# A hybrid encoder's delta rule: one tile per chunk for the loaded keys and the turned b and k

## Chip, cores, metric

One NeuronCore of a Trainium2 chip runs the whole program. The metric is the device time of one execution in microseconds; the table below gives the median of three runs.

## What is computed

The reference is an encoder of two layers over 1,024 tokens with 16 learned meta tokens in front (L = 1040), width 1,024. Each layer has one combined input projection, a latent attention over 4 heads (group A), a delta-rule recurrence over 8 heads of width 64 in both directions (group B), an output projection, a layer norm, and a mixture of 32 experts with a second layer norm. The part that matters here is the recurrence of group B, run once forward and once backward per layer:

```python
def step(S, inp):
    r_t, w_t, k_t, v_t, kk_t, b_t = inp
    sa = jnp.einsum('bhvk,bhk->bhv', S, kk_t)
    S = S * w_t[:, :, None, :] - sa[..., None] * b_t[:, :, None, :] + v_t[..., None] * k_t[:, :, None, :]
    return S, jnp.einsum('bhvk,bhk->bhv', S, r_t)
```

## The kernel before

The program runs layer by layer: input projection, attention, delta rule together with the output projection, router, experts. Everything is float32; products that need full precision are made of three matmuls on rounded halves (`mm3`, L200).

**The delta rule** (`rwkv`, L1449) works in chunks of 64 positions. The padded sequence has 17 chunks, and 4 pairs of heads lie on the two halves of the 128 partitions. A step of the recurrence is one chunk in one direction. `steps` (L1715) takes the directions in turn: forward chunk 0, backward chunk 16, forward chunk 1, and so on, 34 steps in the first layer and 33 in the second. Two neighbouring steps, one of each direction, are a **job** (L1717), 17 jobs per layer. The jobs' products don't depend on the recurrence; they have four stages:

- `grams` (L1479) loads T (keys kk and r, decayed) and BK (b and k) of both chunks from DRAM on SP's DMA queue (L1493, L1495, L1498), and makes the products of BK and T on TensorE (L1509), two PSUM tiles "e" for each chunk. VectorE masks one half of each product back into the other half of T (L1514); ScalarE copies the other half into AA (L1515). GpSimd masks the part AR of AA (L1521). ScalarE scales BK (L1524), TensorE turns it (L1528), and ScalarE copies the result into BT (L1529).
- `blocks` (L1532) inverts the diagonal 16x16 blocks of A on VectorE, mostly for two jobs at a time.
- `levels` (L1563) joins the blocks to the whole inverse Y (L1578 to L1602).
- `chain` (L1619) is the recurrence itself, step after step: T times the ring tile (L1640, and L1647 for the output), Y times that (L1658), copies into the ring (L1659, L1660), BT times the ring for the next state (L1664), the state into the next ring (L1667), and AR times the ring into the output (L1671), which L1674 or L1676 adds up in `yt`. `new_ring` (L1607) loads a ring tile's values four steps ahead.

**Buffers.** T lives in pools rwt0 and rwt1, AA and BT in rws0 and rws1, each with two buffers; jobs 0, 1, 4, 5, ... use the first pair of pools, jobs 2, 3, 6, 7, ... the second. So job j+4 takes the T, AA and BT tiles of job j, and the first instruction that writes into such a tile waits for the last readers of the tile of before: for T these are L1640 and L1647 of job j, for BT L1664, for AA L1671 and `levels`. One T tile holds both chunks of a job (128 x 2 x 4 x 2 x 128 float32, 8 KB per partition). BK has two buffers in a pool of its own. The "e" tiles have two buffers in PSUM, and the output projection that runs beside the delta rule (`attended`, L951, matmuls at L201 to L203, results taken at L969 and L992) uses the same two.

**Order.** The loop of L1742 issues, for each j, the chain of job j, the levels of job j+1, the grams of job j+3, the blocks, and one or two portions of the output projection. That order gives priorities; a planner in the compiler, with its own model of every instruction's time, then fixes each engine's order (L1772). It lets a later stage's instruction go ahead where it takes the earlier ones to be not ready. On the chip each engine and each DMA queue works through its fixed order, so an instruction that waits holds up what stands behind it on its engine. The experts' stage has an order written by hand (L1404) and is not touched.

Of the kernel before, what the change touches and what calls it, by code (L numbers as in the profile page):

```python
# [11 lines left out]
F32 = mybir.dt.float32  # L12
# [3 lines left out]
AF = mybir.ActivationFunctionType  # L16
OP = mybir.AluOpType
# [1431 lines left out]
def rwkv(tc, li, last, K, P, pc, kr_d, bk_d, bon_d, g_dram, vt_d, yT, mhalf, kept, side, ready):  # L1449

    nc = tc.nc
    V = nc.vector
# [9 lines left out]
    HALF = (lo, hi)  # L1462

    def bank():
        return pp.tile([128, 512], F32, name="m")
# [13 lines left out]
    def grams(runs, sv):  # L1479


        U = 4 * sum(n for _, _, n in runs)

        T = sv[0].tile([128, U, 2, 128], F32, name="T")
        BK = kb.tile([128, U, 2, 64], F32, name="BK")

        at, u0 = [], 0
        for d, c0, n in runs:
            us = slice(u0, u0 + 4 * n)
            at += [(d, c0 + u // 4, u % 4) for u in range(4 * n)]  # L1490
            u0 += 4 * n
            for o, h in enumerate(HALF):
                nc.sync.dma_start(T[h, us, o], kr_d[d, h, c0:c0 + n].rearrange("p c i x -> p (c i) x"))  # L1493
            cs = bk_d[d, :, c0:c0 + n].rearrange("p c i (a t) -> p (c i) a t", a=2)
            nc.sync.dma_start(BK[lo, us], cs[lo])  # L1495
            for a in range(2):

                nc.sync.dma_start(BK[hi, us, 1 - a], cs[hi, :, a])  # L1498
        AA = sv[1].tile([128, U, 128], F32, name="AA")
        A, AR = AA[:, :, :64], AA[:, :, 64:]  # L1500
        BT = sv[1].tile([128, U, 2, 64], F32, name="BT")


        for q0 in range(0, U, 4):
            q = slice(q0, q0 + 4)
            ps = [pe.tile([128, 4, 128], F32, name="e") for _ in HALF]
            for u in range(4):
                for o, h in enumerate(HALF):
                    nc.tensor.matmul(ps[o][:, u], BK[h, q0 + u].rearrange("p a t -> p (a t)"), T[h, q0 + u, o],  # L1509
                                     start=True, stop=True)  # L1510
            mask = K(f"mask{at[q0][0]}")
            for o in range(2):
                a, b = HALF[o], HALF[1 - o]
                V.tensor_tensor(T[b, q, o], ps[o][b], mask[b, None, :].to_broadcast([64, 4, 128]), op=OP.mult)  # L1514
                nc.scalar.activation(AA[a, q], ps[o][a], AF.Copy)  # L1515
        u0 = 0
        for d, c0, n in runs:
            us = slice(u0, u0 + 4 * n)
            u0 += 4 * n
            m = K("rev") if d else K("mask0")[:, 64:]  # L1520
            nc.gpsimd.tensor_tensor(AR[:, us], AR[:, us], m[:, None, :].to_broadcast([128, 4 * n, 64]), op=OP.mult)  # L1521

        for u in range(U):
            nc.scalar.activation(BK[:, u], BK[:, u], AF.Copy, scale=pc[:, at[u][0], at[u][2], at[u][1]:at[u][1] + 1])  # L1524
        for q0 in range(0, U, 4):
            ps = bank().rearrange("p (a b) -> p a b", a=4)
            for u in range(4):
                nc.tensor.transpose(ps[:, u], BK[:, q0 + u].rearrange("p a t -> p (a t)"), ident)  # L1528
            nc.scalar.activation(BT[:, q0:q0 + 4].rearrange("p u o x -> p u (o x)"), ps, AF.Copy)  # L1529
        return T, A, AR, BT, {x: u for u, x in enumerate(at)}  # L1530

    def blocks(As, E):  # L1532
# [74 lines left out]
    def new_ring(d, c):  # L1607

        rings[d, c] = ring = ch.tile([128, 4, 2, 64], F32, name="ring", bufs=AHEAD + 2)
        for o in range(2):  # L1610
            nc.sync.dma_start(ring[HALF[1 - o], :, o],
                              vt_d[64 * c:64 * c + 64].rearrange("p (i o x) -> p i o x", i=4, o=2)[:, :, o])
        if c == orders[d][0]:
            for o in range(2):
                nc.gpsimd.memset(ring[HALF[o], :, o], 0.0)
# [1 line left out]
    shared = {}  # L1617

    def chain(job, s, Y):  # L1619
        T, _, AR, BT, units = s  # L1620
        for d, c in job:
            ring = rings.pop((d, c))
            x = steps.index((d, c))
            if x + AHEAD < len(steps):
                new_ring(*steps[x + AHEAD])
            more = c != orders[d][-1]
            want = not (last and c == 0)
            pos = orders[d].index(c)

            def un(i):  # L1630
                return units[d, c, i]


            if x % 2 == 0:
                shared["tu"] = pq.tile([128, 2, 4, 64], F32, name="tu")
                shared["st"] = pq.tile([128, 2, 4, 64], F32, name="st")
            tu, ps = shared["tu"][:, x % 2], shared["st"][:, x % 2]
            for i in range(4):
                for o in range(2):
                    nc.tensor.matmul(tu[HALF[o], i], T[:, un(i), o, 0:64], ring[:, i, o], start=True, stop=True)  # L1640
            t0 = ch.tile([128, 4, 64], F32, name="t0", bufs=2)
            nc.scalar.activation(t0, tu, AF.Copy)
            if want:
                py = pq.tile([128, 4, 64], F32, name="y", bufs=2)
                for i in range(4):
                    for o in range(2):
                        nc.tensor.matmul(py[HALF[o], i], T[:, un(i), o, 64:], ring[:, i, o], start=i == 0, stop=False,  # L1647
                                         skip_group_check=True)
            if more:
                nring = rings[d, orders[d][pos + 1]]  # L1650
                sp = ch.tile([128, 4, 64], F32, name="sp", bufs=2)
                for o in range(2):
                    a = HALF[o]
                    nc.gpsimd.tensor_tensor(sp[a], ring[a, :, o], pc[a, d, :, c:c + 1].to_broadcast([64, 4, 64]),  # L1654
                                            op=OP.mult)
            for i in range(4):
                for o in range(2):
                    nc.tensor.matmul(tu[HALF[o], i], Y[HALF[o], un(i)], t0[HALF[o], i], start=True, stop=True)  # L1658
            nc.scalar.activation(ring[lo, :, 0], tu[lo], AF.Copy, scale=-1.0)  # L1659
            nc.scalar.activation(ring[hi, :, 1], tu[hi], AF.Copy, scale=-1.0)  # L1660
            if more:
                for i in range(4):
                    for o in range(2):
                        nc.tensor.matmul(ps[HALF[o], i], BT[:, un(i), o], ring[:, i, o], start=True, stop=True)  # L1664
                for o in range(2):
                    a = HALF[o]
                    V.tensor_tensor(nring[a, :, o], ps[a], sp[a], op=OP.add)  # L1667
            if want:
                for i in range(4):
                    for o in range(2):  # L1670
                        nc.tensor.matmul(py[HALF[o], i], AR[HALF[o], un(i)], ring[HALF[o], i, o], start=False,  # L1671
                                         stop=True, skip_group_check=True)
                if c in touched:
                    V.tensor_tensor(yt[:, c], yt[:, c], py, op=OP.add)  # L1674
                else:
                    nc.scalar.activation(yt[:, c], py, AF.Copy)  # L1676
                touched[c] = touched.get(c, 0) + 1
                tile_ = [0] if c == 0 else [(c - 1) // 2 * 2 + 1, (c - 1) // 2 * 2 + 2]
                if all(touched.get(x, 0) == 2 for x in tile_):
                    ends.append(tile_)  # L1680
# [39 lines left out]
    def stage(k, j):  # L1720
        if j < len(jobs):
            job = jobs[j]
            if k == 0:
                cs = [sorted(c for d, c in job if d == e) for e in range(2)]
                gs[j] = grams([(d, c[0], len(c)) for d, c in enumerate(cs) if c], svs[j % 4 // 2])
            elif k == 1:
                js = [0] if j == 0 else [x for x in (j, j + 1) if j % 2 and x < len(jobs)]
                if js:
                    Ys.update(zip(js, blocks([gs[x][1] for x in js], V if j == 0 else nc.gpsimd)))
            elif k == 2:  # L1730
                levels(gs[j][1], Ys[j])
            else:
                chain(job, gs.pop(j), Ys.pop(j))
# [42 lines left out]
```

## Time and profile before

| | |
|---|---|
| median of 3 runs | 3237.86 us (3231.32 to 3243.92) |
| the profiled execution | 3243.99 us, span 3242.1 us |
| TensorE matmul busy | 2737.0 us, 84% of the span |
| VectorE busy | 2174.9 us, 67% |
| ScalarE busy | 1658.0 us, 51% |
| GpSimd busy | 1040.8 us, 32% |
| mean granted TensorE clock | 0.881 of full speed |

The profile is of one execution. PE is TensorE's matmul, PEld its weight loads, DVE VectorE, ACT ScalarE, POOL GpSimd, SPq the DMA queue of SyncE. A busy TensorE is not one at its peak, since the matmuls' ends are modelled. Times within the trace are microseconds from the span's start; the first layer's delta rule runs from about 631 to 1122, the second's from about 2240 to 2722. A name in brackets behind a row, as [1.18 <-DMA T<-kr_d], is the engine's idle time just before it and what ended it.

### The profile page before, as it was taken

What the parts mean: (1) busy time and instruction counts of PE and PEld (TensorE: products, weight loads), DVE (VectorE), ACT (ScalarE), POOL (GpSimd) and SP (SyncE); (2) the same over time, 40 slices, a digit from 0 to 9 for tenths busy, and PEclk for the clock granted to TensorE, in tenths of its full rate; (3) what the DMA queues carried; (4) which work ended last, traced back from release to release, by engine and by line L of the source; (5) the groups of instructions that cost most, each with busy time, mean ns of one, the idle gap of its engine ahead of it and who ended that gap; (6) DMA issues with size and microseconds to landing.
All of it is one profiled execution on the core that took longest, in us unless ns stands there. A gap on an engine that the chain in (4) does not pass through costs nothing. (4 is left out here: it accounts for less than half of the span.)

```text
span 3242.1 us, 57910 instructions
## 1 busy us (share of the span) xinstructions
PE 2737.0 (84%) x22160; PEld 2231.9 (69%) x22160; DVE 2174.9 (67%) x4257; ACT 1658.0 (51%) x3604; POOL 1040.8 (32%) x1049
## 2 busy tenths in 40 slices
PE   5989899979998978888498997999699889788882
PEld 4878687768776765666388876888587767566551
DVE  7667554566677668888656747445666666787885
ACT  5334454544445447777433435445344434577772
POOL 3656211143336411111245632112433544111111
PEclk9999899968978979999799988988787879799996
DMA  5345610233323449999724565102432325688875
GB/s 175 103 144 174 200 35 21 66 108 105 91 78 96 144 176 327 323 318 314 252 70 136 161 205 182 40 14 75 130 101 67 95 81 185 235 310 313 309 278 223
DMA packets 342732, 523.76 MB, mean 162 GB/s; under 512 B 110733, under 2 KB 263309, under 8 KB 315809
## 3 DMA queue, kind: packets, MB, share of 16 engines
q1 hardware_dynamic: 234832, 399.11, 38.2%
q10 hardware_dynamic: 93280, 87.04, 7.9%
q0 software_dynamic: 14336, 33.84, 2.9%
q8 instruction: 176, 2.88, 0.4%
q14 instruction: 108, 0.88, 0.1%
HBM read 406.57 MB, written 129.84 MB: 165 GB/s over the span
## 5 line engine op out<-in xcount | busy, mean ns | idle before, releaser
L1221 DVE TENSOR_TENSOR w_lo<-raw,w_hi 128x512 fp32r<-128x512 f32 x768 | 472.8, 684 | 9.3 <-ACT w_hi L1217 9.1
L1217 ACT ACTIVATE w_hi<-raw 128x512 fp32r<-128x512 f32 x768 | 412.1, 620 | 0.0
L201 PE MATMUL pj<-hT_hi,w_hi 128*128 128x352 f32 (+1 forms) x912 | 303.3, 333 | 3.7 <-ACT k L437 2.7
L202 PE MATMUL pj<-hT_lo,w_hi 128*128 128x352 f32 (+1 forms) x912 | 301.4, 331 | 2.8 <-DVE hT_lo L212 2.8
L203 PE MATMUL pj<-hT_hi,w_lo 128*128 128x352 f32 (+1 forms) x912 | 299.7, 329 | 0.0
L1273 POOL DMA_INDIRECT y_rows<-y,VS x64 | 64.5, 1007 | 617.6 <-ACT y L1272 595.7
L201 PE MATMUL ph<-w_hi,xT_hi 128*96 128x512 f32 x512 | 226.9, 443 | 3.4 <-ACT w_hi L1217 3.4
L202 PE MATMUL ph<-w_lo,xT_hi 128*96 128x512 f32 x512 | 222.7, 435 | 1.3 <-DVE w_lo L1221 1.3
L203 PE MATMUL ph<-w_hi,xT_lo 128*96 128x512 f32 x512 | 221.4, 432 | 0.0
L1509 PE MATMUL e<-T,BK 64*128 64x128 f32 x1072 | 171.8, 340 | 38.3 <-DMA T<-kr_d 21.0
L212 DVE TENSOR_TENSOR pT_lo<-tr,pT_hi 128x512 fp32r<-128x512 f32 (+2 forms) x176 | 101.4, 592 | 127.5 <-ACT pT_hi L209 127.0
L201 PEld LDWEIGHTS pj<-hT_hi,w_hi 128*128 128x128 f32 x912 | 176.6, 194 | 14.6 <-issue 6.9
L202 PEld LDWEIGHTS pj<-hT_lo,w_hi 128*128 128x128 f32 x912 | 176.6, 194 | 9.3 <-issue 4.9
L1509 PEld LDWEIGHTS e<-T,BK 64*128 64x128 f32 x1072 | 145.0, 234 | 54.1 <-ACT AA L1515 19.8
L203 PEld LDWEIGHTS pj<-hT_hi,w_lo 128*128 128x128 f32 x912 | 176.1, 193 | 5.0 <-issue 4.3
L1514 DVE TENSOR_TENSOR T<-e,cc 64x512 f32<-64x512 f32 x134 | 92.2, 688 | 89.3 <-PE e L1509 86.9
L1654 POOL TENSOR_TENSOR sp<-ring,pc 64x256 f32<-64x256 f32 x126 | 85.2, 676 | 165.9 <-DVE ring L1667 145.1
L209 ACT ACTIVATE pT_hi<-tr 128x512 fp32r<-128x512 f32 (+2 forms) x176 | 86.7, 517 | 94.3 <-PE tr L873 92.9
L1551 DVE TENSOR_TENSOR sb<-sb,dg 128x16 f32<-128x16 f32 (+8 forms) x270 | 107.1, 397 | 40.5 <-POOL dg L1543 33.4
L203 PEld LDWEIGHTS ph<-w_hi,xT_lo 128*96 128x96 f32 x512 | 93.1, 182 | 43.1 <-issue 3.2
L201 PEld LDWEIGHTS ph<-w_hi,xT_hi 128*96 128x96 f32 x512 | 93.4, 182 | 42.5 <-ACT w_hi L1217 4.1
L202 PEld LDWEIGHTS ph<-w_lo,xT_hi 128*96 128x96 f32 x512 | 93.1, 182 | 40.2 <-DVE w_lo L1221 2.3
(422 smaller groups left out, 7635.3 us busy)
## 6 DMA issues: line engine op xcount, KB each, us to landing
raw<-in_w_moe_dram SPq DMA_DIRECT2D x192, 1024.0 KB
w_raw<-in_w_in_dram SPq DMA_DIRECT2D x38, 512.0 KB
T<-kr_d SPq DMA_DIRECT2D x134, 128.0 KB
ys<-y_rows SPq DMA_DIRECT2D x16, 1024.0 KB
a_d<-ht SPq DMA_DIRECT2D x25, 512.0 KB
h_rows<-h ACTq DMA_DIRECT2D x24, 512.0 KB
kr_d<-KR ACTq DMA_DIRECT2D x16, 576.0 KB
bk_d<-BK ACTq DMA_DIRECT2D x16, 576.0 KB
```

Source lines behind the costliest of these rows:

```text
L201: nc.tensor.matmul(o, a.hi, b.hi, start=start, stop=False)
L202: nc.tensor.matmul(o, a.hi, b.lo, start=False, stop=False)
L203: nc.tensor.matmul(o, a.lo, b.hi, start=False, stop=stop)
L209: hi = nc.scalar.activation(dst.hi, src, AF.Copy)
L212: return hi, e_lo.tensor_tensor(dst.lo, src, dst.hi.bitcast(F32), op=OP.subtract)
L1217: nc.scalar.activation(w.hi[:, cs], raw[:, cs], AF.Copy)
L1221: V.tensor_tensor(w.lo[:, cs], raw[:, cs], w.hi[:, cs].bitcast(F32), op=OP.subtract)
L1273: nc.gpsimd.indirect_dma_start(out=rows, out_offset=bass.IndirectOffsetOnAxis(ap=vs, axis=0), in_=y[:n], in_offset=None, bounds_check=2 * ...
L1509: nc.tensor.matmul(ps[o][:, u], BK[h, q0 + u].rearrange("p a t -> p (a t)"), T[h, q0 + u, o], start=True, stop=True)
L1514: V.tensor_tensor(T[b, q, o], ps[o][b], mask[b, None, :].to_broadcast([64, 4, 128]), op=OP.mult)
L1551: V.tensor_tensor(sb[:, :, cs], sb[:, :, cs], dg[:, :, t_:t_ + 1].to_broadcast([128, n, w]), op=OP.mult)
L1654: nc.gpsimd.tensor_tensor(sp[a], ring[a, :, o], pc[a, d, :, c:c + 1].to_broadcast([64, 4, 64]), op=OP.mult)
```

## The change

T and BT become dictionaries with one tile for each chunk, each of half the size of before, and each of these tiles has four buffers in its pool where there were two. The memory taken is the same. Each chunk's two loads of T go to its own tile. BK, AA and Y stay as they are, one tile for the two chunks of a job. The products, masks, copies and the chain are the same instructions on the new tiles.

```diff
@@ grams
-        T = sv[0].tile([128, U, 2, 128], F32, name="T")
+        T, BT = {}, {}
         BK = kb.tile([128, U, 2, 64], F32, name="BK")
...
-            for o, h in enumerate(HALF):
-                nc.sync.dma_start(T[h, us, o], kr_d[d, h, c0:c0 + n].rearrange("p c i x -> p (c i) x"))
+            for c in range(c0, c0 + n):
+
+                T[d, c] = sv[0].tile([128, 4, 2, 128], F32, name="T", bufs=4)
+                for o, h in enumerate(HALF):
+                    nc.sync.dma_start(T[d, c][h, :, o], kr_d[d, h, c])
...
         AA = sv[1].tile([128, U, 128], F32, name="AA")
         A, AR = AA[:, :, :64], AA[:, :, 64:]
-        BT = sv[1].tile([128, U, 2, 64], F32, name="BT")
...
+            Tq = T[at[q0][:2]]
             for u in range(4):
                 for o, h in enumerate(HALF):
-                    nc.tensor.matmul(ps[o][:, u], BK[h, q0 + u].rearrange("p a t -> p (a t)"), T[h, q0 + u, o],
+                    nc.tensor.matmul(ps[o][:, u], BK[h, q0 + u].rearrange("p a t -> p (a t)"), Tq[h, u, o],
                                      start=True, stop=True)
...
-                V.tensor_tensor(T[b, q, o], ps[o][b], mask[b, None, :].to_broadcast([64, 4, 128]), op=OP.mult)
+                V.tensor_tensor(Tq[b, :, o], ps[o][b], mask[b, None, :].to_broadcast([64, 4, 128]), op=OP.mult)
...
-            nc.scalar.activation(BT[:, q0:q0 + 4].rearrange("p u o x -> p u (o x)"), ps, AF.Copy)
+            bt = BT[at[q0][:2]] = sv[1].tile([128, 4, 2, 64], F32, name="BT", bufs=4)
+            nc.scalar.activation(bt.rearrange("p u o x -> p u (o x)"), ps, AF.Copy)
@@ chain
-        T, _, AR, BT, units = s
+        Ts, _, AR, BTs, units = s
         for d, c in job:
+            T, BT = Ts[d, c], BTs[d, c]
...
-                    nc.tensor.matmul(tu[HALF[o], i], T[:, un(i), o, 0:64], ring[:, i, o], start=True, stop=True)
+                    nc.tensor.matmul(tu[HALF[o], i], T[:, i, o, 0:64], ring[:, i, o], start=True, stop=True)
...
-                        nc.tensor.matmul(ps[HALF[o], i], BT[:, un(i), o], ring[:, i, o], start=True, stop=True)
+                        nc.tensor.matmul(ps[HALF[o], i], BT[:, i, o], ring[:, i, o], start=True, stop=True)
```

## Rows read from the trace of the kernel before

**Rows 1.** Windows of both stages: us; busy (count) of PE, PEld, DVE, ACT, POOL; clock, DMA
```profile
631.40:1122.00 490.60, 434.89 (x6257) 359.76 (x6256) 338.29 (x880) 225.51 (x520) 205.03 (x214) 0.85 0.34 96
2240.00:2722.00 482.00, 421.81 (x5943) 352.85 (x5941) 314.99 (x849) 214.09 (x498) 193.11 (x206) 0.82 0.34 95
```

**Rows 2.** TensorE's waits, first stage then second: us in total, times, longest
```profile
PE tu L1640 <- DMA ring<-vt_d: 10.5, 1, 10.5
PE e L1509 <- DMA T<-kr_d: 10.0, 7, 2.5
PE e L1509 <- ACT AA L1515: 7.8, 8, 2.6
...
PE tu L1640 <- DMA ring<-vt_d: 16.4, 1, 16.4
PE e L1509 <- DMA T<-kr_d: 10.9, 6, 2.4
PE e L1509 <- ACT AA L1515: 9.5, 7, 3.7
```

**Rows 3.** Timeline of TensorE within one job: start, us, instructions of one kind merged
```profile
719.03 1.12 PE L1647 MATMUL y<-ring,T 128*64 128x64 f32 x16
...
738.97 0.56 PE L1647 MATMUL y<-ring,T 128*64 128x64 f32 x10
739.58 0.33 PE L1664 MATMUL st<-ring,BT 128*64 128x64 f32 x2
...
741.34 1.93 PE L1509 MATMUL e<-T,BK 64*128 64x128 f32 x8 [1.18 <-DMA T<-kr_d]
...
743.87 1.11 PE L1664 MATMUL st<-ring,BT 128*64 128x64 f32 x14
744.92 1.11 PE L1671 MATMUL y<-ring,AA 64*64 64x64 f32 x14
...
746.42 1.12 PE L1640 MATMUL tu<-ring,T 128*64 128x64 f32 x16
```

**Rows 4.** Timeline of SP's DMA queue before and in the same job
```profile
703.02 0.47 SPq L1495 DMA_DIRECT2D BK<-bk_d  x1
...
733.24 0.52 SPq L1495 DMA_DIRECT2D BK<-bk_d  x1
...
737.79 3.38 SPq L1493 DMA_DIRECT2D T<-kr_d  x4
```

**Rows 5.** Timeline of ScalarE in the same job
```profile
746.35 0.58 ACT L1515 ACTIVATE AA<-e 64x512 f32<-64x512 f32 x1
...
753.82 0.60 ACT L1529 ACTIVATE BT<-m 128x512 f32<-128x512 f32 x1 [0.26 <-PE m L1528]
...
758.92 0.38 ACT L1660 ACTIVATE ring<-tu 64x256 f32<-64x256 f32 x1
```

**Rows 6.** Windows around three waits for T, columns as in rows 1
```profile
740.20:741.30 1.10, 0.00 (x0) 0.00 (x0) 1.07 (x4) 0.00 (x0) 0.00 (x0) 1.00 0.62 183
...
741.30:762.00 20.70, 20.66 (x189) 17.43 (x190) 14.54 (x37) 9.24 (x22) 5.72 (x6) 0.51 0.28 74
...
888.40:903.00 14.60, 14.58 (x160) 12.69 (x161) 6.46 (x21) 5.54 (x13) 2.13 (x3) 0.50 0.10 26
938.90:950.00 11.10, 11.10 (x140) 9.89 (x140) 6.39 (x17) 4.54 (x11) 2.11 (x3) 0.53 0.18 44
```

**Rows 7.** Timeline of TensorE behind a wait for L1515
```profile
800.67 1.16 PE L1509 MATMUL e<-T,BK 64*128 64x128 f32 x8 [1.39 <-ACT AA L1515]
...
803.36 1.86 PE L1509 MATMUL e<-T,BK 64*128 64x128 f32 x7
```

**Rows 8.** SP's own waits from 700 to 1020: us in total, times, longest
```profile
SPq L1493 <- PE tu L1658: 4.0, 5, 1.3
```

**Rows 9.** Timeline of TensorE, side work ahead of the chain (first of 24, then L1664)
```profile
758.21 0.79 PE L201 MATMUL e<-wo_hi,ya_hi 128*128 128x512 f32 x1
...
765.62 0.69 PE L1664 MATMUL st<-ring,BT 128*64 128x64 f32 x16
```

More of the change, by code (lines that the diff above doesn't have):

```diff
@@ L1646, in chain @@
                     for o in range(2):
-                        nc.tensor.matmul(py[HALF[o], i], T[:, un(i), o, 64:], ring[:, i, o], start=i == 0, stop=False,
+                        nc.tensor.matmul(py[HALF[o], i], T[:, i, o, 64:], ring[:, i, o], start=i == 0, stop=False,
                                          skip_group_check=True)
```

## The prediction

> **What bounds the kernel now.** The chain of waits that ended last only shows the last stage, so I read the delta-rule stages by windows first. There are two, one per layer, 490.6 and 482.0 us long, together 30% of the span; TensorE is busy 89% and 88% of them at a mean granted clock of 0.85 and 0.82 [rows 1]. All else in the program is left as it is. So the change can only win or lose here: TensorE's idle time is 490.6 - 434.9 = 55.7 and 482.0 - 421.8 = 60.2 us, and a clock below 1.
>
> Next the waits of TensorE in these stages [rows 2]. The largest single ones are the first ring loads (10.5 and 16.4 us, once per layer), which no part of the change touches. Then comes what it does touch: the key products of L1509 wait for the load of T, 10.0 us in 7 waits and 10.9 us in 6, together 20.9 us. The same products wait 7.8 and 9.5 us for L1515, which empties their PSUM bank into AA.
>
> Third, one job in order of time. T of job j is last read by L1647 of its second chunk (start 738.97, sixteen matmuls) [rows 3]. The four loads of T for job j+4 start on SP at 737.79 and take 3.38 us, the first of them held up [rows 4]. L1509 starts at 741.34 after 1.18 us of idle TensorE, eight matmuls at 1.93 us; the recurrence's own L1664 of the same step, which had begun at 739.58, goes on only at 743.87, and the next job's L1640 follows at 746.42 [rows 3]. So the load is issued when the old T tile comes free and is used at once: here the buffer, not the transfer's length, sets the time. The other operand is early: BK for these products was loaded from 703.02 on, and 733.24 is already the next job's [rows 4].
>
> **The change, part by part.** *Counts:* 134 loads of T, the products, masks and copies stay; only what they wait for differs. No instruction is added and none is longer, so the direct cost is nil on every queue.
>
> *T.* The first chunk's T is free when L1647 of the first chunk ends, start 719.03 plus 1.12 [rows 3], instead of about 739.5: 19 us earlier. Its two loads can go out on SP in the stretch before the BK loads of 733.24 [rows 4]. L1509 of that chunk then finds T in place, and the 13 waits go: -20.9 us at most [rows 2]. The second chunk's T still comes free at 739.5, but only two loads instead of four are issued then, and its products run behind the first chunk's, at 747 or later in this job, well after they land. I cost that at nothing; the cover is the first chunk's products and, if these have already run, the wait would be back, 1.6 us each (20.9/13).
>
> *What is late next.* L1515 writes AA, still one tile for two chunks with two buffers. It can't start before L1671 of the second chunk, 744.92 plus 1.11, and it does start at 746.35 [rows 3, 5]. So the products' results leave PSUM no earlier, and the second half of the products meets the wait for L1515, whose present mean is 17.3/15 = 1.15 us [rows 2]. I let half of the 13 jobs pay it: 6 x 1.15 = +7. Net -14 us. The ends: -21 (none pays), and 0 (each pays as much as it saved).
> The Trainium skill ("Perfetto Trace Analysis", the section Optimization Strategy) reads a gap that keeps coming back on the engine that should be busy as a sign of too few or too large buffers for the next tile; by that rule alone the smaller T tiles would give back the whole 20.9 us, and the sum would be 7 us lower than mine. The rows show a second tile, AA, with the same users and the same two buffers, which the rule doesn't set against the first; so I keep the +7.
>
> *TensorE's clock.* In the gap of 740.2 to 741.3 the granted clock is 1.00 with nothing running; in the 20.7 us behind it, 0.51, with TensorE busy throughout; 14.6 us at 0.50 and 11.1 at 0.53 follow two other waits of this kind [rows 6]. That is the 1.2 GHz level. At the 2.4 GHz level these three stretches would lose up to half, 10 + 7 + 5 = 22 us, if TensorE's work alone set their length. The ends for the clock are 0 and about -50 us, this sum carried to seven of the 13 waits (22 x 7/3 = 51). But the clock falls behind waits that stay, too: after 1.39 us for L1515 at 800.67, seven products at 803.36 take 1.86 us [rows 7]. I take -10, nearer to nothing because the wait for L1515 is still there.
>
> *SP.* The early load of the first chunk can stand in SP's order ahead of BK, ring and y loads. If L1647 runs late, these wait behind it. SP's waits for T now are 4.0 us in 5 cases [rows 8]; BK is 30 us early and rings are four steps ahead, so nothing of that reaches TensorE. *BT.* Its copy starts at 753.82 [rows 5], behind L1664 of both chunks at 743.87; an earlier release of half of it moves nothing: 0. *First loads of a stage and the last releases:* the first products wait for the attention's end, not for T: 0.
>
> Sum against the profiled execution, 3243.99 us (span 3242.1 and 1.9 around it): -14 - 10 = -24, 3220. The median of the runs is 6.1 us lower, so **3214 us**.
>
> **The rivals.**
> *The wait only moves (no difference).* AA's release at 746 stays the tightest tie, and the order that the planner writes down is fixed for the run: with the wait for T gone, TensorE waits for L1515 in the same gap. For it: L1515 follows L1671 by 1.4 us in this job [rows 3, 5]. Against: in the gap at 740.2, L1664 of the chain stands behind the products, and that goes with T alone. Time: 3238 less 0 to 8, about 3234.
>
> *Early products hold the PSUM banks (slower).* Products of a chunk take both "e" banks, and keep them until L1515, which waits for AA. Today they start about 5 us ahead of AA's release; with T free at 720 they can start up to 20 us ahead. The output projection's side work needs the same two banks; two halves, 24 matmuls, run from 758.21 to 765.62, 3.7 us per half, and there they already stand ahead of the chain's L1664, whose input was ready at 759.3 (758.92 plus 0.38) [rows 5, 9]. If a half that now fills a gap is pushed behind AA's release, it lies on the chain. With one half in every second of 28 jobs that is 14 x 3.7 = +52, less the 24 saved: +28, 3266. It decides from about seven halves on (24/3.7). For it: two banks and three users. Against: the side work of an earlier round is ordered ahead of later products wherever both are ready.
> The Trainium skill ("Trainium Kernel Development and Optimization", Best Practices) warns to mind PSUM pressure, since evacuation is not made faster by what speeds up the matmuls; that is this rival, and no row yet shows the banks as the cause of a late projection.
>
> *The clock comes back in full (much faster).* The gaps go and with them most half-speed stretches: -14 - 36 = -50, 3188. For it: TensorE is busy in the whole of each such stretch. Against: the fall behind a wait that stays [rows 7].
>
> **How the numbers follow.** Forecast 0.42, no difference 0.27, banks held 0.20, full clock 0.11. About 0.5% (16 us) is what a measurement of this kernel can tell from no change. The forecast's own range is 3204 to 3228; a sixth of its chance, 0.07, lies within 0.5%. Faster: 0.35 + 0.11 = 0.46. Same: 0.27 + 0.07 = 0.34. Slower: 0.20. The range begins at the full-clock case, 3187, and ends at 3258, seven tenths of the way from 3238 to the slower case; the rest of that case and a little below 3187 are left out.
>
> **What would show it.** Right: TensorE's waits of L1509 for T fall from 20.9 us to under 4; the two T loads of a job's first chunk are issued apart from the second's, some 15 us earlier; L1664 of a second chunk is no longer cut in two by products; the stages are 470 to 480 us long with a clock of 0.86 or more. Wrong: the waits for L1515 grow from 17.3 to 30 us or more (the wait moved); the side work of L201 to L203 stands later in its job and waits for L1515 (banks held); or the waits for T stay, with the second chunk's products now first behind their load. A changed order far from T, such as longer first ring waits, would make the prediction wrong for a reason that it doesn't hold.

## The result, and the profile after

The changed kernel takes 3213.12 us (median of 6 runs, 3206.73 to 3217.06), the kernel before 3240.89 us (median of 6, 3231.32 to 3253.51). The ratio is 0.9911 with a 95% interval of 0.9888 to 0.9934, so it is faster by 0.9%, by more than the 0.5% that can be told from no change. The profiled execution took 3206.73 us, its span 3205.0 us, at a mean granted clock of 0.897 (before: 3243.99, 3242.1 and 0.881).

The windows of both stages after the change (length; busy time and count of PE, PEld, DVE, ACT, POOL; clock, DMA share, GB/s):

```profile
633.00:1108.00 475.00, 411.44 (x6203) 339.39 (x6202) 331.41 (x863) 220.55 (x515) 200.22 (x212) 0.87 0.34 96
2235.00:2682.00 447.00, 381.87 (x5907) 317.38 (x5907) 309.81 (x844) 208.80 (x486) 192.38 (x204) 0.89 0.36 101
```

Against [rows 1] the windows are 15.6 and 35.0 us shorter and the clock is up from 0.85 and 0.82; they do not hold quite the same work (6203 matmuls against 6257, and 5907 against 5943). But TensorE's idle time, length less PE busy, is 63.6 and 65.1 us where it was 55.7 and 60.2. The change was to remove idle time, and there is more of it; the busy time fell.

To compare kernels I narrow the windows to the recurrence itself, from the first to the last T-times-ring product (L1640 before, L1645 after) of each layer; the first ring load's wait lies ahead of it. First the kernel before:

```profile
669.60:1108.00 438.40, 397.24 (x5932) 328.08 (x5932) 300.95 (x785) 196.69 (x458) 181.71 (x191) 0.85 0.35 99
2284.00:2721.90 437.90, 394.18 (x5736) 328.87 (x5736) 282.60 (x764) 191.00 (x445) 175.90 (x186) 0.83 0.34 98
```

The same windows after:

```profile
673.70:1099.60 425.90, 379.45 (x5932) 312.51 (x5932) 298.24 (x785) 195.37 (x458) 179.72 (x191) 0.87 0.34 98
2271.90:2678.90 407.00, 359.65 (x5734) 298.33 (x5736) 281.08 (x763) 189.64 (x446) 176.12 (x186) 0.90 0.36 103
```

The counts of matmuls agree within two, so it is the same work. Together the two windows fell from 876.3 to 832.9 us (-43.4): PE busy from 791.4 to 739.1 (-52.3), idle from 84.9 to 93.8 (+8.9). The rest of the program was 6.3 us longer in this execution (2372.1 against 2365.8), which makes the span's 37.1. The execution profiled after the change is the fastest of its six, so this is more than the medians' 27.8 us.

TensorE's waits after the change in the two stages, first then second (us in total, times, longest):

```profile
PE e L1512 <- ACT AA L1518: 9.3, 8, 3.8
PE y L1652 <- DVE ring L1672: 7.5, 4, 5.0
PE y L1652 <- DVE yt L1679: 5.8, 4, 3.3
PE y L1652 <- ACT AA L1518: 2.0, 1, 2.0
PE m L1603 <- ACT W L1599: 1.2, 3, 0.5
...
PE y L1652 <- DVE yt L1679: 11.0, 5, 8.0
PE e L1512 <- ACT AA L1518: 8.7, 7, 3.2
PE m L1603 <- ACT W L1599: 7.6, 7, 5.6
PE y L1652 <- ACT AA L1518: 2.8, 3, 1.2
PE y L1652 <- DVE ring L1672: 2.0, 3, 0.9
```

No wait for T is left where there were 20.9 us of them [rows 2]. The key products (L1512 now) wait 18.0 us for L1518, practically the 17.3 of before. What grew are the waits of the output product and the levels, which in the kernel before stood as follows (first stage, then second):

```profile
PE y L1647 <- DVE yt L1674: 5.6, 4, 3.2
PE m L1599 <- ACT W L1595: 0.7, 2, 0.5
...
PE y L1647 <- DVE yt L1674: 6.5, 4, 2.6
PE y L1647 <- DVE ring L1667: 2.7, 1, 2.7
PE m L1599 <- ACT W L1595: 2.3, 3, 1.6
```

The output product waited 5.6 + 6.5 + 2.7 = 14.8 us for VectorE and now waits 7.5 + 5.8 + 11.0 + 2.0 = 26.3; the levels' wait for W went from 3.0 to 8.8. These two groups alone take back 17.3 of the 20.9 us. Another 4.8 us of the output product's waits are put down to L1518, and none were before.

One job of the first layer, at the place of [rows 3], on TensorE after the change (start, length, merged instructions, idle time before):

```profile
739.61 0.56 PE L1652 MATMUL y<-ring,T 128*64 128x64 f32 x10
740.10 1.16 PE L1512 MATMUL e<-T,BK 64*128 64x128 f32 x16
...
741.71 0.68 PE L1669 MATMUL st<-ring,BT 128*64 128x64 f32 x14
...
743.54 0.69 PE L1645 MATMUL tu<-ring,T 128*64 128x64 f32 x16
746.20 1.05 PE L1652 MATMUL y<-ring,T 128*64 128x64 f32 x16 [1.97 <-ACT AA L1518]
747.17 2.38 PE L1512 MATMUL e<-T,BK 64*128 64x128 f32 x16
```

The same place on SP's queue:

```profile
721.99 1.84 SPq L1496 DMA_DIRECT2D T<-kr_d  x2
...
738.45 1.91 SPq L1496 DMA_DIRECT2D T<-kr_d  x2
```

Each chunk has its own pair of loads. Counted from the start of the stage, the products at 740.10 are the eleventh chunk's and use the eleventh pair, 721.99 to 723.83, there 16 us earlier; those at 747.17 are the twelfth chunk's and use the pair that ended at 740.36, 7 us earlier. Before, the four loads ended at 741.17 and the products began at 741.34 [rows 3, 4]. Sixteen records of products (the trace has two for each matmul, so this is one chunk's eight) now take 1.16 us without a gap, where eight records took 1.93 at the lower clock, and the next job's first product starts at 743.54, not 746.42 [rows 3]. Then a wait of another kind comes, 1.97 us at 746.20. It is put down to L1518, though L1652 doesn't read AA; by the same timeline L1672 writes the ring tile that it reads from 745.64 on, 0.87 us in two halves. The clock around it (columns as in the windows above):

```profile
739.50:746.00 6.50, 4.73 (x113) 4.02 (x108) 6.15 (x19) 3.49 (x9) 0.56 (x1) 1.00 0.58 157
746.00:754.80 8.80, 8.53 (x76) 7.30 (x77) 8.24 (x22) 4.95 (x13) 4.76 (x6) 0.62 0.11 32
754.80:760.00 5.20, 5.20 (x37) 3.92 (x35) 3.65 (x7) 1.35 (x3) 0.69 (x2) 0.99 0.21 50
```

Where [rows 6] had 20.7 us at 0.51 there are now 8.8 us at 0.62. The clock still falls behind a wait, but later and for less.

### The profile page after: what moved, and what is told of

Same layout as the page of the kernel before. It is cut to its first block, busy times and chain, and to the rows that moved or that the text cites. A ratio compares the mean times of both kernels' runs of the same rounds, so it can differ in the third digit from the quotient of the medians.

```text
span 3205.0 us, 57957 instructions
## 1 busy us (share of the span) xinstructions
PE 2675.5 (83%) x22160; PEld 2177.7 (68%) x22160; DVE 2172.9 (68%) x4257; ACT 1653.0 (52%) x3604; POOL 1040.0 (32%) x1049
## 5 line engine op out<-in xcount | busy, mean ns | idle before, releaser
L201 PE MATMUL pj<-hT_hi,w_hi 128*128 128x352 f32 (+1 forms) x912 | 303.3, 333 | 3.7 <-ACT k L437 2.7
L201 PE MATMUL ph<-w_hi,xT_hi 128*96 128x512 f32 x512 | 226.1, 442 | 3.4 <-ACT w_hi L1217 3.4
L201 PEld LDWEIGHTS pj<-hT_hi,w_hi 128*128 128x128 f32 x912 | 176.7, 194 | 14.9 <-issue 6.9
L1512 PE MATMUL e<-T,BK 64*128 64x128 f32 x1072 | 150.7, 320 | 19.4 <-ACT AA L1518 18.0
L1512 PEld LDWEIGHTS e<-T,BK 64*128 64x128 f32 x1072 | 125.7, 215 | 33.1 <-ACT AA L1518 20.6
L1517 DVE TENSOR_TENSOR T<-e,cc 64x512 f32<-64x512 f32 x134 | 92.3, 689 | 59.3 <-PE e L1512 56.4
L201 PEld LDWEIGHTS ph<-w_hi,xT_hi 128*96 128x96 f32 x512 | 93.1, 182 | 42.4 <-issue 4.7
```

The lines of the kernel that those rows point to most:

```text
L201: nc.tensor.matmul(o, a.hi, b.hi, start=start, stop=False)
L1517: V.tensor_tensor(Tq[b, :, o], ps[o][b], mask[b, None, :].to_broadcast([64, 4, 128]), op=OP.mult)
```

## The experiments

Three questions: is it T's tie or BT's, or merely another order (the planner writes a new order for every kernel); is AA the next tie; and is it the idle time or the clock that pays. A chip's own median of before ran from 3254.81 to 3262.77 us in these runs, so ratios to before on the same chip are compared. All results in one table. *Recurrence*, *PE busy* and *idle* are sums over the two windows of each profiled execution; *lower level* is worked out as twice the length times (1 - clock), since every record of the granted clock stands at one of two levels, 1.0 or half of it (as the clock is read with two digits, this is good to about 9 us); *T waits* are TensorE's in the whole program.

| run | ratio to before (95%) | recurrence | PE busy | idle | clock | lower level | T waits |
|---|---|---|---|---|---|---|---|
| before | 1 | 876.3 | 791.4 | 84.9 | 0.85, 0.83 | 280 | 21.0 |
| after | 0.9911 (0.9888 to 0.9934) | 832.9 | 739.1 | 93.8 | 0.87, 0.90 | 192 | 0 |
| after_again | 0.9880 (0.9852 to 0.9909) | 836.8 | 744.5 | 92.3 | 0.87, 0.89 | 201 | 0 |
| t_only | 0.9895 (0.9835 to 0.9956) | 831.1 | 743.8 | 87.3 | 0.86, 0.90 | 200 | 0 |
| bt_only | 1.0018 (0.9990 to 1.0047) | 873.2 | 796.0 | 77.2 | 0.83, 0.83 | 297 | 18.9 |
| tied | 0.9974 (0.9942 to 1.0007) | 868.9 | 791.9 | 77.0 | 0.83, 0.84 | 287 | 16.0 |
| tied_own | 0.9942 (0.9916 to 0.9968) | 847.0 | 758.4 | 88.6 | 0.86, 0.87 | 229 | 0 |
| aa_chunk | 0.9867 (0.9835 to 0.9899) | 818.2 | 742.9 | 75.3 | 0.90, 0.88 | 180 | 0 |
| aa_chunk_again | 0.9866 (0.9837 to 0.9895) | 819.5 | 744.9 | 74.6 | 0.91, 0.88 | 172 | 0 |
| aa_only | 0.9992 (0.9967 to 1.0017) | 858.5 | 774.4 | 84.1 | 0.86, 0.85 | 249 | 15.7 |
| side_m | 1.0052 (1.0028 to 1.0077) | 863.4 | 755.3 | 108.1 | 0.80, 0.80 | 345 | 0 |
| before_fill | 1.0000 (0.9978 to 1.0021) | 894.8 | 807.0 | 87.8 | 0.84, 0.87 | 260 | 3.7 |
| before_fill_again | 0.9994 (0.9974 to 1.0014) | 874.3 | 780.0 | 94.3 | 0.89, 0.87 | 210 | 1.3 |
| after_fill | 1.0050 (1.0030 to 1.0070) | 898.3 | 811.4 | 86.9 | 0.87, 0.84 | 260 | 0 |

The columns behind the ratio come from a single execution each. Where a kernel was profiled twice, the recurrence differs by 3.9 us (after), 1.3 us (aa_chunk) and 20.5 us (before_fill), so a difference of that size between two rows shows little by itself. In the aa_chunk and the fill kernels, and in side_m, the windows hold another number of matmuls than in the rest.

**Half of the change each.** `t_only` has T in tiles for each chunk and BT in one for the job; `bt_only` the reverse. Against the changed kernel:

```diff
# t_only
+        BTj = sv[1].tile([128, U, 2, 64], F32, name="BT")
...
-            bt = BT[at[q0][:2]] = sv[1].tile([128, 4, 2, 64], F32, name="BT", bufs=4)
+            bt = BT[at[q0][:2]] = BTj[:, q0:q0 + 4]
# bt_only
+        Tj = sv[0].tile([128, U, 2, 128], F32, name="T")
...
-                T[d, c] = sv[0].tile([128, 4, 2, 128], F32, name="T", bufs=4)
+                T[d, c] = Tj[:, us]
```

Expected of `t_only`:

> One T tile for each chunk, BT again one tile for a job. Theory (T's earlier release is the whole gain): 3205 to 3222 us, as the changed kernel's 3213; the waits of the key products for T are gone. Rival (BT's earlier release carries it): about 3240. Rival (any new order of the instructions gives some gain or loss): anywhere from 3195 to 3255.

Expected of `bt_only`:

> One BT tile for each chunk, T again one tile for a job. Theory (BT costs and gives nothing): within 8 us of the kernel before (3241), TensorE's waits for T still some 21 us in 13 cases. Rival (BT carries the gain): about 3213. Rival (any new order gives some gain or loss): more than 15 us off the kernel before, with the waits for T unchanged.

Measured: 3217.82 us (4 runs), ratio 0.9895, and 3259.45 us (10 runs), 1.0018. T alone carries the change; BT is worth nothing that can be told from no change. The kernel of `bt_only` has a new order of its own and its T tied, as has `aa_only` below (0.9992), and neither is off the kernel before.

**The tie put back.** `tied` is the changed kernel with a small addition in GpSimd in each job's second step, which reads the first chunk's T and a value of the second step's T-times-ring, so that the first chunk's T is released late again. `tied_own` has the same addition on the second chunk's own T. The sum is used by nothing.

```diff
             nc.scalar.activation(t0, tu, AF.Copy)
+            if x % 2:
+                tie = ch.tile([128, 16], F32, name="tie", bufs=1)
+                nc.gpsimd.tensor_tensor(tie, Ts[job[0]][:, 0, 0, 0:16], t0[:, 0, 0:16], op=OP.add)   # tied
+                nc.gpsimd.tensor_tensor(tie, T[:, 0, 0, 0:16], t0[:, 0, 0:16], op=OP.add)            # tied_own
```

Expected of `tied`:

> The changed kernel with one small GpSimd addition in each job's second step that reads 16 columns of the first chunk's T and the second step's t0: the first chunk's T comes free about 18 us later again, nearly as late as before; the tiles stay one for each chunk. Theory (the moment of T's release is what counts): 3228 to 3245 us, waits for T back at 10 us or more, clock of the stages back to about 0.84. Rival (the smaller tiles' new order or the shorter burst of loads is what counts): 3205 to 3222.

Expected of `tied_own`:

> The control of the run before: the same small addition in the same place, but it reads the second chunk's own T, so the first chunk's T is released as early as in the changed kernel. Theory: 3208 to 3222 us, waits for T near zero. If the addition itself or the new order is what moves the time: like the run with the tie, 3228 or more.

Measured on one chip, ten runs each: 3250.71 us (3239.07 to 3262.22) with the tie, 3234.39 (3226.55 to 3237.97) without. Both lie above the ranges expected, which were written for a chip where the kernel before takes 3240.89 us; the ratios make 3232.5 and 3222.1 of them there, the first inside its range and the second at the edge of its own. The slowest run of the control is below the fastest of the tied kernel, though the intervals of the two ratios overlap. TensorE's waits of the tied kernel and its windows:

```profile
PE e L1512 <- DMA T<-kr_d: 16.0, 11, 3.7
```

```profile
677.00:1119.20 442.20, 406.13 (x5932) 335.39 (x5932) 300.97 (x785) 197.45 (x458) 186.30 (x207) 0.83 0.33 94
2301.80:2728.50 426.70, 385.80 (x5735) 322.42 (x5736) 285.93 (x763) 189.27 (x445) 179.84 (x202) 0.84 0.35 100
```

The windows of the control:

```profile
677.90:1106.70 428.80, 386.26 (x5930) 317.44 (x5932) 297.05 (x786) 194.89 (x458) 184.44 (x207) 0.86 0.35 97
2294.60:2712.80 418.20, 372.13 (x5735) 309.14 (x5736) 285.99 (x764) 190.09 (x445) 180.71 (x202) 0.87 0.36 102
```

With the tie the waits for T are back, 16.0 us in 11. The idle time is smaller by 11.6 us (77.0 against 88.6) and yet the recurrence takes 21.9 us more, because the same matmuls are busy for 33.5 us more at a lower clock. The control itself, at 0.9942, lost a part of the change's gain: an addition that ties nothing, or the order that came with it, costs some 0.3 to 0.6%. So much a new order may do here.

**AA, too, for each chunk.** `aa_chunk` gives AA four half-size tiles; `aa_only` does that with T in one tile for the job (AA and BT for each chunk). `blocks` and `levels` then read AA chunk by chunk, so GpSimd has more and shorter instructions (1113 against 1049).

```diff
-        AA = sv[1].tile([128, U, 128], F32, name="AA")
-        A, AR = AA[:, :, :64], AA[:, :, 64:]
+        AA = [sv[1].tile([128, 4, 128], F32, name="AA", bufs=4) for _ in range(U // 4)]
+        A = [x[:, :, :64] for x in AA]
+        AR = {at[4 * k][:2]: x[:, :, 64:] for k, x in enumerate(AA)}
...
```

Expected of `aa_chunk`:

> The changed kernel with AA, too, as one tile for each chunk with four buffers, so that its first half is released a chunk earlier; GpSimd has 68 more, shorter multiplications. Two theories. (a) The waits that TensorE has left for L1518 (9.3 us in 8 and 8.7 us in 7 of the changed kernel) are of the same kind as those for T were, and each is followed by a stretch at the lower clock: the waits fall to under 6 us together, the mean clock of the two stages rises by 0.02 or more, and the ratio to the kernel before is 0.980 to 0.986, below the change's 0.991. (b) With T untied, TensorE is held by the recurrence itself (ring, y and m waits), and the waits for AA are only where it happens to stand: another wait takes their place, and the ratio stays at 0.989 to 0.994. If the clock follows the number of waits rather than their length, (a) holds even if only half the 18 us go.

Expected of `aa_only`:

> AA and BT one tile for each chunk with four buffers, T one tile for the two chunks of a job as before. If the T tie itself sets the time, T's waits stay at 15 to 21 us and the ratio to the kernel before is 0.995 to 1.003 whatever AA does. If T and AA are two ties of the same worth, the AA waits fall from 17.3 us to under 8 and the ratio is 0.990 to 0.995. If the gain of the change is only a luckier order, which any edit of these tiles may bring, the ratio may be anything from 0.988 to 1.005, with no relation to the waits for T.

And of the repetition beside the changed kernel:

> The kernel with T, BT and AA in tiles for each chunk again, beside the changed kernel on one chip. If the waits for AA were worth something of their own once T's were gone, its ratio is 0.983 to 0.989 and its time 0.3% or more below the changed kernel's beside it; if the first reading (0.9867) was chance, the two agree within 0.2%.

> The changed kernel again, on the chip of the next run, so that the two can be set against each other: ratio 0.989 to 0.994 by either theory.

Measured: `aa_chunk` 0.9867 and 0.9866, the changed kernel beside it 0.9880; on that chip 3216.99 against 3222.23 us, 0.16%, inside the 0.2% that was to mean no difference. Its recurrence is 17.3 us shorter in the two profiles of that chip (836.8 less 819.5), but the rest of the program varies by as much between executions (2372.1 us in the first profile of the changed kernel, 2392.2 in the second), and of the two executions profiled there one is the changed kernel's slowest (3230.78 us), the other lies 9 us below its median. So a gain over the change is not shown. Nor is either theory met as it was written: the key products' waits for the copy (L1519 here) are 15.8 us and not under 6, and the ratio lies between the two ranges. `aa_only`, with T's waits at 15.7 us, is at 0.9992: untying AA is worth nothing while T is tied, and the key products' waits for the copy did not fall (19.8 us, after 17.3). In its one profile the recurrence is 17.8 us shorter than in the kernel before and the rest of the program 31.1 us longer; why is open. What ScalarE's copy into AA waits for, in the kernel before, and the instruction ahead of the copy of [rows 5]:

```profile
ACT AA L1515 <- DVE T L1514: 37.8, 44, 3.7
ACT AA L1515 <- PE y L1671: 14.3, 3, 6.0
...
746.07 0.38 ACT L1676 ACTIVATE yt<-y 128x256 f32<-128x256 f32 x1 [6.14 <-PE y L1671]
```

In the changed kernel:

```profile
ACT AA L1518 <- DVE T L1517: 56.4, 58, 7.3
ACT AA L1518 <- PE y L1676: 4.0, 4, 1.3
```

With AA in tiles for each chunk, ScalarE and then TensorE:

```profile
ACT AA L1519 <- DVE T L1518: 46.6, 50, 2.8
ACT AA L1519 <- PE y L1680: 2.9, 2, 2.3
...
PE e L1513 <- ACT AA L1519: 15.8, 13, 5.1
```

The release of the old AA by the output products held the copy in 3 cases before and in 4 after. In 44 and 58 cases the copy waited for VectorE's mask, which empties the other half of the same products. These counts can miss a case: the copy at 746.35 [rows 5] shows no wait of its own, for it stands behind L1676, which had waited 6.14 us for the same L1671. The stronger ground is `aa_chunk`: with smaller AA tiles the wait is still 15.8 us, so AA's tie is not what makes up most of it.

**The projection on other PSUM banks.** `side_m` is the changed kernel with the output projection on the "m" banks.

```diff
-    side = side(lambda: pe.tile([128, 512], F32, name="e"))
+    side = side(bank)
```

Expected:

> The changed kernel with the output projection's products moved from the two "e" banks of PSUM to the banks "m", which the turns and the levels use. The rival of banks held: if early products keep the projection out of the "e" banks in the changed kernel, this gives 5 to 20 us back: ratio 0.985 to 0.990. If the banks don't matter, as the 2.5 us of waits of L201 for L1518 in the changed kernel say, the ratio is that of the change within the order's spread, 0.989 to 0.996; a worse one, over 0.996, would mean that the "m" banks are the scarcer ones.

Measured: 1.0052, slower than both kernels. It has the lowest clock of all runs and the most idle time:

```profile
677.30:1113.80 436.50, 378.80 (x5848) 314.15 (x5848) 298.16 (x772) 195.03 (x455) 176.28 (x188) 0.80 0.32 88
2305.10:2732.00 426.90, 376.52 (x5652) 313.64 (x5652) 279.88 (x751) 190.88 (x444) 168.83 (x182) 0.80 0.32 90
```

The key products' wait for L1518 fell from 18.0 to 10.6 us, but 84 and 82 matmuls moved out of the two windows, and the levels, which share the "m" banks, waited more; the largest of their waits, 9.3 us in 8 in the changed kernel, is now

```profile
PE m L1596 <- DVE X L1589: 30.3, 18, 7.8
```

The expectation took a ratio over 0.996 to mean that the "m" banks are the scarcer ones. That is not shown: the wait is put down to VectorE's transpose, not to a bank. The run took a load off the "e" banks and put it on others, so of the banks' rival it says only that this way gives nothing back.

**Work in the gap.** `before_fill` is the kernel before, and `after_fill` the changed kernel, with eight more products of BK with itself ahead of the key products of each job's first chunk, in the same bank, where the real ones overwrite them. They need no T.

```diff
             ps = [pe.tile([128, 4, 128], F32, name="e") for _ in HALF]
+            if q0 == 0:
+                for u in range(4):
+                    for o, h in enumerate(HALF):
+                        k = BK[h, u].rearrange("p a t -> p (a t)")
+                        nc.tensor.matmul(ps[o][:, u], k, k, start=True, stop=True)
```

Expected of `before_fill`:

> The kernel before with eight more products of BK with itself ahead of the key products of each job's first chunk, into the same PSUM bank, overwritten by the real ones; they wait for BK and the bank, not for T. So TensorE does something in the gap in which it waited for T. The added work is 34 x 8 products, 33 us at the full clock (half of 1.93 us for eight) and 66 us at the half one, where nothing covers it. If the idle gap is what the clock falls behind, and the clock is the price of the waits, the stages' mean clock rises from 0.85 and 0.82 to 0.87 or more and the ratio is 0.995 to 1.008: the added work is paid back by the clock. If the clock does not depend on the gap, it stays at 0.82 to 0.85 and only the covered part is free (13 gaps of some 1.6 us hold eight products each, 13 to 21 us): the ratio is 1.008 to 1.018.

Of `after_fill`:

> The changed kernel with the same eight additional products ahead of the key products of each job's first chunk as in the run before_fill, where 74 us of them cost nothing (ratio 1.000). If they were free there because they stood in the gaps of the waits for T and kept the clock up, then here, where no wait for T is left, they find no such gap and cost a part of their time: ratio to the kernel before 0.998 to 1.012, that is 0.7 to 2% over the change's own 0.991. If they were free for another reason (a better order, idle time anywhere on TensorE, or a clock that likes any added work), they are free here too: 0.988 to 0.995.

Of `before_fill_again`:

> The run before_fill again: its profiled execution, 3276.06 us, was the slowest of its twelve, 20 us above their median, so the trace and the ratio of 1.000 did not tell the same tale. If the added products are really free in the kernel before, the ratio is 0.996 to 1.004 again, and a profiled execution near the median shows the recurrence of both layers in 870 to 885 us together, with a mean clock of 0.86 or more (0.85 and 0.83 without them). If the profiled execution was the truer one, the ratio is 1.006 or more and the windows again some 895 us.

Measured: in the kernel before 1.0000 and 0.9994, in the changed kernel 1.0050 where the change alone is at 0.9880 on the same chip, 3273.17 against 3222.23 us. The groups of the added and of the real products in `before_fill_again` (count, busy us, mean ns, idle time before them):

```profile
L1514 PE MATMUL e<-T,BK 64*128 64x128 f32 x1072 | 152.5, 327 | 17.2 <-ACT AA L1520 15.7 <-DMA T<-kr_d 1.3
L1511 PE MATMUL e<-BK 64*128 64x128 f32 x544 | 75.0, 326 | 3.3 <-DVE ht L969 3.2
```

Its busy times on the page, and its windows:

```profile
PE 2729.5 (84%) x22704; PEld 2232.2 (69%) x22704; DVE 2168.6 (67%) x4257; ACT 1651.9 (51%) x3604; POOL 1040.7 (32%) x1049
```

```profile
681.10:1122.60 441.50, 393.13 (x6156) 328.22 (x6156) 294.90 (x791) 192.79 (x457) 180.27 (x193) 0.89 0.34 96
2292.50:2725.30 432.80, 386.83 (x5959) 323.35 (x5959) 287.23 (x777) 190.19 (x450) 177.40 (x190) 0.87 0.35 99
```

The added products of the changed kernel:

```profile
L1514 PE MATMUL e<-BK 64*128 64x128 f32 x544 | 76.2, 330 | 3.4 <-DVE ht L969 1.1 <-ACT AA L1523 0.9 <-DVE ht L992 0.9
```

75.0 us of useless products cost the kernel before nothing, and 76.2 us of the same cost the changed kernel 51 us. The expectation's 33 us at the full clock took the eight records of 1.93 us for eight products; they are four, so its figure should have been 66. In the kernel before the added products cover the waits for T (21.0 us to 1.3), which is far from 75. In the second profile the rest came from the clock: with 544 more matmul records TensorE is busy for 2729.5 us in all, where the kernel before has 2737.0, at 0.89 and 0.87 in the windows instead of 0.85 and 0.83. Idle time was not saved (94.3 us in the windows against 84.9). The first profile doesn't show as much: in it TensorE is busy for 2765.5 us, and the clock is 0.84 in the first window, no rise, and 0.87 in the second. That execution, at 3276.06 us, was the slowest of its twelve; the second, at 3252.5 us, lies 6 us below its median.

## Why the prediction was right, and which of its terms were not

The time, 3214 predicted and 3213.12 measured, and the sign were right. The sum behind it was not: it took -14 us from idle time and -10 from the clock, and the profile has +9 of idle time and -52 of busy time in the recurrence, and +6 elsewhere. Two wrong terms and one that was not thought of cancel, so that the time came out within 1 us is luck. In the changed kernel's second profile PE busy is 744.5 us and idle time 92.3, much the same.

- **T: right, though two rows were misread.** The waits for T are gone entirely, loads go out by chunk, and they land 16 and 7 us ahead of their products in the job looked at. `t_only` and `bt_only` show that T is the part that counts, and `tied` that it is the late release. The products' gap in the recurrence's L1664 [rows 3] is gone: L1669's fourteen matmuls follow its first two with only L1676 between. The misreading is in who reads T last. Counted from the start of the stage, L1647 at 719.03 and 738.97 [rows 3] belongs to the fourth and the fifth step, so the second of them is the next job's, and the load at 737.79 [rows 4] starts ahead of it. The last readers of the two chunks' T are L1640 of the third and the fourth step:

```profile
714.08 1.12 PE L1640 MATMUL tu<-ring,T 128*64 128x64 f32 x16
...
736.26 0.69 PE L1640 MATMUL tu<-ring,T 128*64 128x64 f32 x16
```

So the first chunk's T was free at 715.20 and the second's at 736.95, 22 us apart, where the prediction had 19; the argument stands.
- **What is late next: wrong.** The step priced +7 for L1515 on the ground that AA's release at 744.92 plus 1.11 stays. The key products' waits for L1518 rose by 0.7 us only, and AA's release was not their main cause: ScalarE is seen waiting for VectorE's mask, and `aa_chunk` leaves the wait near where it was. Counted over the output product and the projection too, what is put down to L1518 rose from 18.5 to 25.3 us, near the +7 in size, but not by the products or the release that the step names. Mostly the output product and the levels wait longer for others, +17.3 us in the two groups shown. The first ring waits, which the prediction set aside, grew as well, from 26.9 to 30.3 us. A TensorE that runs faster through the same job meets VectorE and ScalarE earlier, and their busy time did not fall (windows: DVE 583.6 to 579.3, ACT 387.7 to 385.0). That this is the reason, and not the new order, was not tested.
The Trainium skill ("Perfetto Trace Analysis", Optimization Strategy) takes a recurring gap as a sign of too few or too large buffers. For the gap itself that held: the smaller T tiles took all 20.9 us of it. It puts no price on a gap, and the 20.9 us were not the price here: TensorE's idle time is larger than before, and the gain came in elsewhere.
- **The clock: the right mechanism, the wrong size.** I took -10 of a range of 0 to -50, since the clock falls behind other waits, too. Measured: PE busy -52.3 us for the same matmuls, the end of that range. The time at the lower level fell from about 280 to 192 us. The trace of before could have priced it. In the 21 us behind each of the 13 waits for T the clock is 0.51 to 0.59 in seven cases where no other long wait follows, as in the first of these rows, and 0.92 to 1.00 in five, as in the second (the thirteenth is mixed with other waits):

```profile
2347.40:2368.40 21.00, 20.92 (x198) 17.66 (x199) 12.30 (x30) 9.24 (x22) 5.84 (x7) 0.59 0.25 68
...
840.70:861.70 21.00, 19.65 (x334) 16.36 (x336) 18.56 (x47) 11.12 (x28) 8.55 (x10) 1.00 0.37 103
```

These seven hold some 130 us at the lower level, nearly half of the 280, and seven is the number that the prediction's end of -50 was carried to. Since the total fell by less, about 88, some of it came back behind other waits. The argument for a small figure, that a wait that stays brings the clock down as well, is true [rows 7], as the window at 746 shows again, but the stretch there is shorter: 8.8 us at 0.62 against 20.7 at 0.51.
- **BT and SP at nothing: right.** `bt_only` is at 1.0018, and no wait for BK or for a load of T is among TensorE's first ones. The load at 738.45 is the second chunk's. It goes out 0.9 us after the last reader of its tile,

```profile
736.90 0.69 PE L1645 MATMUL tu<-ring,T 128*64 128x64 f32 x16
```

so nothing shows that SP's order held it up.
- **The rivals.** "The wait only moves" named a true effect, with the wrong successor, and left out that the lower clock does not move with it. "The clock comes back in full" was nearest in mechanism; it took -36 from the clock, where -52 was measured, and its -14 from the gaps was not met. The signs named for a right forecast were met but for one length: the stages were to be 470 to 480 us long, and the windows are 475.0 and 447.0. "Banks held" has nothing for it: L201 waits 2.6 us for L1518 in the whole program, after 1.2.

What remains open. In the runs the recurrence's length goes with the time at the lower level, not with the idle time (of the kernels with the same matmuls in the windows: 280 and 297 us for 876 and 873, 249 for 859, 229 for 847, 192 to 201 for 831 to 837; `tied`, at 287, has 869). The direction of cause is supported by `before_fill`, whose edit adds nothing but TensorE's activity ahead of the products that waited. But every edit gets another order from the planner, and `tied_own` shows that this may be worth 0.3 to 0.6%. A run with an unchanged order and only the tie cut was not made. Nor was it settled why some waits for T are followed by some 20 us at the lower level and others by none, and why those of the output product mostly have shorter ones behind them.

## What to carry to other kernels

Price a wait of TensorE not by its length but with the stretch at the lower clock that follows it in the trace: here 21 us of waits for one tile, once gone, took some 50 us off the busy time of the same matmuls. And after such a change read PE busy and idle time apart, for a wait that goes can come back in another place and the kernel still be faster.
A tile that two steps share is released by the later one; before splitting it, look which release its writer truly waits for. For T that was the release; for AA, built in the same way, it was not, as far as the runs show.

## What was not expected of the hardware

Useless matmuls in a gap can be free, or nearly so: 75 us of them left the kernel before at 0.9994 and 1.0000. TensorE's busy time, with 544 more matmul records, was 7.5 us shorter in one profile and 28.5 us longer in the other. In the kernel without the gap the same matmuls cost 1.6% (3273.17 against 3222.23 us). And the clock can be worse with no wait for T at all: 0.80 in both windows of `side_m`, whose idle time, 108.1 us, is the largest of all.
